# Hybrid encoder layer with product-key retrieval: bank stores on another queue, merged one-hots, token pairs in the weight bank, and 48 spilled up tiles for 60

## The chip, the cores and the metric

One core of a Trainium2 chip. The metric is the device time of one execution in microseconds; lower is better. Engines are called PE (matrix), DVE (vector), ACT (scalar), POOL (GpSimd) and SP (the engine that only issues transfers).

## What is computed

One layer of an encoder on 512 tokens of width 1,024 with 16 meta tokens in front: differential attention and a bidirectional gated linear attention side by side, an output projection, and then a retrieval block (PEER) over 128 x 128 = 16,384 single-neuron experts. Cut to the block that matters here:

```
q = (xn @ w_q)                       # 8 heads x 2 halves of 128
s = q . sub_keys                     # 128 scores per head and half
ts, ti = top_k(s, 16)                # per half
best = top_k(ts0[:, None] + ts1[None, :], 16)      # 16 of 256 pairs
idx = ti0 * 128 + ti1                # expert of each pair
act = gelu(xn . u[idx])
h = h + sum((softmax(best) * act) * v[idx])
```

followed by a final RMS norm. `u` and `v` are 16,384 x 1,024.

## The kernel before

Everything is float32; large products run as three matmuls on a high and a low half (`mm3`, L126 to L129). The first 128 tokens take the **sparse** way: their 128 (head, rank) pairs are fetched row by row from `u` and `v` by indirect transfers that POOL issues (`gather`, L249; 256 in all), and DVE does a dot product per row of `u` (L265) and a multiply-add per row of `v` (L263). The other 384 tokens (three tiles of 128) take the **dense** way: for each of the 128 blocks of 128 experts an *up tile* computes gelu(`u` block . tokens) with 24 matmuls of 384 columns (`u_tile`, L1044), and a *value tile* multiplies it by the gate weights of that block and accumulates with 18 matmuls of 512 columns into six PSUM banks (`v_tile`, L1065 to L1084). The gate weights of all experts for all 384 tokens are built beforehand as a table, the **weight bank** `W_d` in memory.

The stages, in order: the front (attention, projections), the scores and top-16 searches (`topk2`, L189 to L244), and then

- the **bank stage** (loop at L1122 to L1139): `wbuild` builds the bank while the first LA = 60 up tiles run between its pieces, their gelus spilled to memory as `A_d` (L1057). For 8 tokens at a time `prep` (L970) makes one-hots: `L993` compares the two expert indices of each pair with a row 0..127 (two instructions of 1,024 elements), L994 and L996 multiply the first one-hot with the low and the high half of the gate; in every fourth block ACT makes the high product instead (eight instructions at L999). For each token two matmuls of 128 columns (L1021, L1022) sum the outer products over the 128 pairs; four tokens fill one PSUM bank, and ACT drains it (L1024) into a staging tile `stg` of [128, 128, 32], token innermost. After 32 tokens the 2 MB tile is stored to `W_d` (L1026); there are two staging tiles and four one-hot tiles. GS0, RA, RV and RUV say how many gathers are started per up tile or value tile (`pull`), and LA how many up tiles lie in this stage;
- the **value stage** (L1142 on): 128 value tiles; behind the 60th each is joined by one up tile, so the last 68 come as pairs.

A streamed up block goes SP load (`raw`, two buffers), ACT cast (`hi`, L114), `lo` subtraction (L116; on POOL in the bank stage, on DVE afterwards), PE. Each engine runs its instructions in the order that the scheduler wrote them; POOL's queue holds the `lo` subtractions and the gather issues, SP's all loads and the bank stores:

```
hi = stm.tile([P, 1024], F32R, name="hi", tag="hi", bufs=bufs)              # L113
nc.scalar.copy(hi, raw)                                                     # L114
lo = stm.tile([P, 1024], F32R, name="lo", tag="lo", bufs=bufs)              # L115
(eng or nc.vector).tensor_sub(lo, raw, hi.bitcast(F32))                     # L116
```

The row 0..127 is loaded to `iof` at L949, into space that the score tiles release, and cast to `ioh`.

Of the kernel before, what the change touches and what calls it, by code (L numbers as in the profile page):

```python
# [49 lines left out]
SC = 16  # L50
# [32 lines left out]
def _emit(ctx, tc, I, out):  # L83
# [105 lines left out]
    def topk2(a, b, sm, cand, tf, eq, zs):  # L189
# [758 lines left out]
    iof = wk.tile([P, NK], F32, name="iof")  # L948
    nc.sync.dma_start(out=iof, in_=I["iota"].to_broadcast([P, NK]))  # L949
# [11 lines left out]
    def wbuild():  # L961
# [8 lines left out]
        def prep(t, m0):  # L970
            if m0 == 0:
# [5 lines left out]
                iT = wk2.tile([P, 2, P], F16, name="iT")  # L977
                nc.scalar.copy(iT, tr[:, 1:3, :])
                gh = wk2.tile([P, P], F16, name="gh")
                nc.vector.tensor_copy(gh, gT)  # L980
                gl = wk2.tile([P, P], F16, name="gl")
                nc.vector.tensor_sub(gl, gT, gh)
                cur[t] = gT, iT, gh, gl
            gT, iT, gh, gl = cur[t]
            sh = [P, OB // QI, NK, QI]
# [19 lines left out]
        for n, (t, m0) in enumerate(steps):  # L1005
# [262 lines left out]
```

## Time and profile before

| | |
|---|---|
| three timed runs | 1680.73, 1678.32, 1671.53 us; median 1678.32 |
| the profiled execution | 1682.47 us, span of its instructions 1680.7 us |
| busy share of the span | PE 94%, DVE 77%, ACT 44%, POOL 40% |
| memory traffic | 387.42 MB, mean 231 GB/s |
| bank stage, first to last bank matmul | 566.7 to 814.0 us |
| first value matmul | 846.2 us |

The profile is of one execution. Matmuls are pipelined and their ends are modelled, so the distance from one start to the next tells PE's pace. A row that gives "idle before" names what the engine waited for last.

### The profile page before, as it was taken

To read this page: it belongs to the slowest core of one execution; us is meant where nothing else is said; L and a number is where in the kernel's file an instruction comes from. 1 tells how busy PE (TensorE), PEld (TensorE's weight loads), DVE (VectorE), ACT (ScalarE), POOL (GpSimd) and SP (SyncE) were. 2 spreads that over 40 slices of the span, in tenths; PEclk is the share of its full clock that TensorE was granted. 3 is DMA by queue.
4 is the path that set the end of the run, shared out by engine and by line. 5 is a ranking of instruction groups with operands and counts; after the bars stand their busy time and mean duration, and the time that the engine had idled before them with its cause. 6 is when DMAs were issued, how large, how long until landed. Compare 5 with 4: busy or idle time off the path is not lost.

```text
span 1680.7 us, 24243 instructions
## 1 busy us (share of the span) xinstructions
PE 1574.4 (94%) x8793; PEld 1392.4 (83%) x8793; DVE 1291.4 (77%) x2529; ACT 739.6 (44%) x1229; POOL 677.1 (40%) x465
## 2 busy tenths in 40 slices
PE   6999998989986789979989999999999999999998
PEld 6888886768876689878978888889999999988996
DVE  3888768647999998948247777778887888778777
ACT  5454555543324474867533333333333333333334
POOL 3443112076334467475411212154545444344442
PEclk9999999989997989999999999999999999999999
DMA  6112222232224557656999999899999998999885
GB/s 232 54 46 81 69 61 69 84 118 89 78 73 149 176 193 250 239 218 252 328 366 342 326 314 326 278 313 389 321 329 326 336 327 315 319 339 327 308 276 185
DMA packets 152360, 387.42 MB, mean 231 GB/s; under 512 B 12752, under 2 KB 71376, under 8 KB 150576
## 3 DMA queue, kind: packets, MB, share of 16 engines
q1 hardware_dynamic: 106160, 238.79, 41.2%
q0 software_dynamic: 36864, 134.23, 22.8%
q10 hardware_dynamic: 9216, 12.85, 2.1%
q8 instruction: 69, 1.13, 0.3%
q14 instruction: 51, 0.42, 0.1%
HBM read 342.56 MB, written 40.63 MB: 228 GB/s over the span
## 4 chain that ended last, share of the span: by engine, by line
PE 28%; issue 18%; DVE 12%; POOL 10%; DMA 6%; ACT 3%; SPq 1%; POOLq 0%; ACTq 0%; DVEq 0%
POOL gat L251 7%; PE banka L1080 4%; PE banka L1083 4%; PE banka L1084 4%; POOL lo L116 3%; PE bankp L1080 2%; PE bankp L1083 2%; PE bankp L1084 2%; PE bankg L129 2%; DMA gat<-v,idx 2%; PE bankg L127 2%; PE bankg L128 2%; DMA raw<-uT 2%; DVE oh L993 2%; DMA gat<-u,idx 1%
## 5 line engine op out<-in xcount | busy, mean ns | idle before, releaser
L116 POOL TENSOR_TENSOR lo<-raw,hi 128x1024 fp32r<-128x1024 f32 x81 | 238.4, 2947 | 228.8 <-ACT hi L114 220.4
L114 ACT CAST hi<-raw 128x1024 fp32r<-128x1024 f32 x177 | 185.8, 1051 | 289.6 <-PE bankg L128 159.1
L127 PE MATMUL bankg<-un_hi,hi 128*128 128x384 f32 x880 | 300.1, 341 | 12.2 <-ACT act L1055 12.2
L129 PE MATMUL bankg<-un_hi,lo 128*128 128x384 f32 x880 | 299.6, 341 | 5.3 <-POOL lo L116 5.2
L128 PE MATMUL bankg<-un_lo,hi 128*128 128x384 f32 x880 | 297.9, 338 | 0.0
L251 POOL DMA_INDIRECT gat<-u,idx x128 | 157.8, 1232 | 299.5 <-PE bankp L1084 252.1
L251 POOL DMA_INDIRECT gat<-v,idx x128 | 167.8, 1311 | 207.6 <-PE bankp L1084 180.4
L263 DVE SCALAR_TENSOR_TENSOR acc<-gat,sact,acc 128x1024 f32<-128x1024 f32 x128 | 164.2, 1283 | 72.2 <-DMA gat<-v,idx 61.6
L265 DVE CUSTOM_DVE_ANT_0 gat<-gat,hn 128x1024 f32<-128x1024 f32 x128 | 162.9, 1282 | 53.2 <-DMA gat<-u,idx 53.1
L127 PEld LDWEIGHTS bankg<-un_hi,hi 128*128 128x128 f32 x880 | 168.1, 191 | 16.1 <-ACT act L1055 12.5
L135 DVE TENSOR_TENSOR vhl<-vraw,vhl 128x1024 fp32r<-128x1024 f32 x128 | 157.1, 1228 | 30.9 <-ACT vhl L134 30.8
L129 PEld LDWEIGHTS bankg<-un_hi,lo 128*128 128x128 f32 x880 | 167.9, 191 | 8.1 <-POOL lo L116 6.8
L128 PEld LDWEIGHTS bankg<-un_lo,hi 128*128 128x128 f32 x880 | 167.7, 191 | 3.4
L134 ACT CAST vhl<-vraw 128x1024 fp32r<-128x1024 f32 x128 | 134.2, 1049 | 46.3 <-PE bankp L1084 33.4
L116 DVE TENSOR_TENSOR lo<-raw,hi 128x1024 fp32r<-128x1024 f32 x96 | 117.8, 1228 | 24.2 <-ACT hi L114 23.0
L1024 ACT ACTIVATE stg<-banka 128x512 f32<-128x512 f32 x96 | 96.2, 1140 | 1.7 <-PE banka L1022 0.9
L993 DVE TENSOR_TENSOR oh<-iT,ioh 128x1024 f16<-128x1024 f16 x96 | 80.8, 888 | 2.4 <-PE banka L1022 2.4
L1021 PE MATMUL banka<-oh 128*128 128x128 f16 x384 | 55.3, 233 | 22.1 <-DVE oh L996 12.7
L1055 ACT ACTIVATE act<-bankg 128x384 f32<-128x384 f32 x110 | 53.4, 486 | 23.2 <-PE bankg L129 12.1
L1021 PEld LDWEIGHTS <-oh 128*128 128x128 f16 x384 | 39.2, 104 | 20.8 <-DVE oh L996 15.0
L1022 PE MATMUL banka<-oh 128*128 128x128 f16 x384 | 54.3, 233 | 0.7 <-DVE oh L994 0.7
L129 PE MATMUL bankp<-un_hi,lo 128*128 128x384 f32 x144 | 48.7, 338 | 4.5 <-POOL lo L116 4.5
(2283 smaller groups left out, 3906.3 us busy)
## 6 DMA issues: line engine op xcount, KB each, us to landing
raw<-uT SPq DMA_DIRECT2D x128, 512.0 KB
vraw<-v SPq DMA_DIRECT2D x128, 512.0 KB
W_d<-stg SPq DMA_DIRECT2D x12, 2048.0 KB
wa<-W_d SPq DMA_DIRECT2D x32, 768.0 KB
A_d<-act ACTq DMA_DIRECT2D x60, 192.0 KB
wa<-A_d SPq DMA_DIRECT2D x15, 768.0 KB
raw<-wq SPq DMA_DIRECT2D x16, 512.0 KB
raw<-win_n SPq DMA_DIRECT2D x12, 512.0 KB
```

Of the source, the lines that this page charges most:

```text
L114: nc.scalar.copy(hi, raw)
L116: (eng or nc.vector).tensor_sub(lo, raw, hi.bitcast(F32))
L127: nc.tensor.matmul(o, lhsT=ah, rhs=bh, start=start, stop=False)
L128: nc.tensor.matmul(o, lhsT=ah, rhs=bl, start=False, stop=False)
L129: return nc.tensor.matmul(o, lhsT=al, rhs=bh, start=False, stop=stop)
L134: last[0] = nc.scalar.copy(hi, src).ins.name
L135: (eng or nc.vector).tensor_sub(lo, src, hi.bitcast(F32))
L251: g = nc.gpsimd.indirect_dma_start(out=r, out_offset=None, in_=src, in_offset=bass.IndirectOffsetOnAxis(ap=idx[:, hk:hk + 1], axis=0))
L263: nc.vector.scalar_tensor_tensor(acc0, r, sact[:, hk:hk + 1], acc0, op0=ALU.mult, op1=ALU.add)
L265: nc.vector.tensor_tensor_reduce(r, r, hn0, scale=1.0, scalar=0.0, op0=ALU.mult, op1=ALU.add, accum_out=sact[:, hk:hk + 1])
L993: nc.vector.tensor_tensor(o12[:, j], tok(iT[:, j]), ioh[:, None, :, :].to_broadcast(sh), op=ALU.is_equal)
L1080: m0 = nc.tensor.matmul(o, lhsT=gh_[:, tc_], rhs=vh[:, dc], start=(j == 0), stop=False, skip_group_check=True)
```

## The change

Five edits and four numbers.

1. **Stores.** The twelve stores of `stg` go to ACT's queue instead of SP's.
2. **Index row.** `iof` lives in a tile of its own from the start of the retrieval block, and is loaded ahead of `keys`. The score tiles `sc` lose one buffer (SC 16 to 15).
3. **One-hots.** The two compares become one instruction of 2,048 elements; the gate halves lie beside each other in `gs`, and the low and the high product become one instruction of 2,048 elements, except in every fourth block. In `topk2` the two positions and the row 0..15 are bf16, so the compare reads 16-bit operands only.
4. **Bank.** A PSUM bank holds [2, 128, 2] instead of [4, 128]: two adjacent tokens lie beside each other, so a matmul writes every other word, and the drain writes pairs of adjacent words into `stg`.
5. **Numbers.** RA 0.4 to 0.15, RUV 2.85 to 2.7, LA 60 to 48.

```diff
-SC = 16
+SC = 15
-RA = 0.4
+RA = 0.15
-RUV = 2.85
-LA = 60
+RUV = 2.7
+LA = 48
...
-            nc.vector.tensor_tensor(eq, pos[:, :, :, None].to_broadcast([P, PH, TOPK, TOPK]),
-                                    io16[:, None, None, :].to_broadcast([P, PH, TOPK, TOPK]), op=ALU.is_equal)
+            nc.vector.tensor_tensor(eq, pos[:, :, :, None].to_broadcast([P, PH, TOPK, TOPK]),
+                                    io16b[:, None, None, :].to_broadcast([P, PH, TOPK, TOPK]), op=ALU.is_equal)
...
+    iof = w1.tile([P, NK], F32, name="iof")
+    nc.sync.dma_start(out=iof, in_=I["iota"].to_broadcast([P, NK]))
     keys = qs.tile([P, 2 * PH, NK], F32, name="keys")
...
-            for j in range(2):
-                nc.vector.tensor_tensor(o12[:, j], tok(iT[:, j]), ioh[:, None, :, :].to_broadcast(sh), op=ALU.is_equal)
-            nc.vector.tensor_mul(ol, o12[:, 0], tok(gl))
-            if m0 // OB % DM < DN:
-                nc.vector.tensor_mul(od, o12[:, 0], tok(gh))
+            nc.vector.tensor_tensor(o12, tok(iT[:, blk].rearrange("p j m -> p (j m)")),
+                                    ioh[:, None, :, :].to_broadcast([P, 2 * GQ, NK, QI]), op=ALU.is_equal)
...
+            if blk % DM < DN:
+                nc.vector.tensor_mul(oh[:, 2 * GQ:].rearrange("p (c g) k q -> p c (g k q)", c=2).rearrange("p c (g k q) -> p c g k q", k=NK, q=QI),
+                                     o12[:, None, 0].to_broadcast([P, 2] + sh[1:]),
+                                     gs[:, blk].rearrange("p c (g q) -> p c g q", q=QI)[:, :, :, None, :].to_broadcast([P, 2] + sh[1:]))
             else:
+                nc.vector.tensor_mul(ol, o12[:, 0], tok(gs[:, blk, 1]))
...
-                b = bank((P, 4, NK))
+                b = bank((P, 2, NK, 2))
...
-                    nc.tensor.matmul(b[:, q2, :], lhsT=w_, rhs=od[:, m_[0], :, m_[1]], start=True, stop=False)
-                    nc.tensor.matmul(b[:, q2, :], lhsT=w_, rhs=ol[:, m_[0], :, m_[1]], start=False, stop=True)
+                    nc.tensor.matmul(b[:, q2 // 2, :, q2 % 2], lhsT=w_, rhs=od[:, m_[0], :, m_[1]], start=True, stop=False)
+                    nc.tensor.matmul(b[:, q2 // 2, :, q2 % 2], lhsT=w_, rhs=ol[:, m_[0], :, m_[1]], start=False, stop=True)
                 qq = q0 + 4 * g_
-                nc.scalar.activation(stg[:, :, qq:qq + 4].rearrange("p i n -> p n i"), b, AF.Copy, scale=1.0 / GS)
+                nc.scalar.activation(stg[:, :, qq:qq + 4].rearrange("p i (a n) -> p a i n", n=2), b, AF.Copy, scale=1.0 / GS)
             if q0 + OB == BL:
-                nc.sync.dma_start(out=W_d[:, ((t - 1) * P + m0) // BL], in_=stg)
+                nc.scalar.dma_start(out=W_d[:, ((t - 1) * P + m0) // BL], in_=stg)
```

The scheduler writes the order anew. On SP, from the score weights to the bank stage, `raw<-uT` being the loads of up blocks, before:

```order
L897 DMA keys<-keys 128x2048
L108 DMA raw<-wq 128x1024 x11
L108 DMA raw<-uT 128x1024 x7
L949 DMA iof<-iota 128x128
L108 DMA raw<-uT 128x1024 x14
L1026 DMA W_d<-stg 128x4096
L108 DMA raw<-uT 128x1024 x3
```

and with the change:

```order
L901 DMA iof<-iota 128x128
L903 DMA keys<-keys 128x2048
L108 DMA raw<-wq 128x1024 x11
L108 DMA raw<-uT 128x1024 x47
L1050 DMA vraw<-v 128x1024 x2
L1122 DMA wa<-W_d 128x12x128
```

Nothing stands between the up loads of the bank stage any more; the first loads of the value stage (`vraw`, `wa`) follow them.

On ACT the first store of the bank now stands behind the drains (`stg`) and ahead of the next gelu (`act`) and cast (`hi`):

```order
L1066 ACTIVATE act<-bankg 128x384
L1035 ACTIVATE stg<-banka 128x2x128x2 x2
L1068 DMA A_d<-act 128x384
L1035 ACTIVATE stg<-banka 128x2x128x2 x6
L1037 DMA W_d<-stg 128x4096
L1066 ACTIVATE act<-bankp 128x384
L114 CAST hi<-raw 128x1024
```

On DVE, at the start of the bank stage, the one-hots (`oh`), an index chain (`eq`) and uses of gathered rows (`gat`), before:

```order
L993 TENSOR_TENSOR oh<-iT,ioh 128x1024 x7
L996 TENSOR_TENSOR oh<-oh,gh 128x1024
L994 TENSOR_TENSOR oh<-oh,gl 128x1024
L265 ISA gat,sact<-gat,hn_70 128x1024
L265 ISA sact 128x1
L994 TENSOR_TENSOR oh<-oh,gl 128x1024
L996 TENSOR_TENSOR oh<-oh,gh 128x1024
```

and with the change:

```order
L234 TENSOR_TENSOR eq<-sm_cb,io16b 128x2048
L228 TENSOR_TENSOR sm_cf<-sm_cf,sm_bsv 128x128
L230 TENSOR_SCALAR sm_rf<-sm_rf 128x128
L985 CAST gs<-gT 128x16x8
L999 TENSOR_TENSOR oh<-iT,ioh 128x2048 x4
L236 TENSOR_TENSOR eq<-eq,tf 128x2048
L229 TENSOR_TENSOR sm_cb<-sm_cf,sm_t_6099 128x128
L231 TENSOR_TENSOR sm_rb<-sm_rf,sm_t_6099 128x128
L986 TENSOR_TENSOR gs<-gT,gs 128x16x8
L237 TENSOR_TENSOR eq<-eq 128x128x8
L1004 TENSOR_TENSOR oh<-oh,gs 128x2048 x3
L1008 TENSOR_TENSOR oh<-oh,gs 128x1024
```

Half as many one-hot instructions do the same elements; four uses of gathered rows stand in this stage instead of sixteen, and the third of the four index chains has moved ahead of the first one-hot but for its second half. On PE the new order has 410 up matmuls ahead of the first bank matmul, 598 between it and the last, and 144 behind that; before, the 144 were the same and the first two numbers 377 and 919.

## Rows read from the trace of the kernel before

**Rows 1.** Busy time by stage: stretch, its length, then busy us (and instructions) of PE, its weight loads, DVE, ACT and POOL, the granted clock of PE, the DMA share and GB/s. The stretches are the bank stage, the way to the first value matmul, and the value stage up to and behind the point where pairs begin.

```profile
566.70:814.10 247.40, 216.76 (x1670) 207.06 (x1669) 202.62 (x231) 171.06 (x268) 149.88 (x52) 0.95 0.65 233
814.10:846.10 32.00, 25.15 (x147) 24.83 (x144) 5.25 (x6) 10.50 (x16) 10.41 (x5) 0.96 0.99 349
846.10:1124.50 278.40, 278.32 (x1241) 232.61 (x1242) 204.05 (x297) 101.94 (x141) 60.68 (x58) 0.99 0.93 321
1124.50:1672.70 548.20, 545.39 (x2769) 494.70 (x2767) 441.80 (x523) 193.58 (x278) 246.78 (x183) 1.00 0.90 318
```

**Rows 2.** PE in order of time: start, duration, line, operation and tiles, count, and in brackets the idle time before it with what ended it. All bank matmuls between the third and the fourth row follow without a gap.

```profile
508.82 0.69 PE L127 MATMUL bankg<-un_hi,hi 128*128 128x384 f32 x1 [12.16 <-ACT act L1055]
...
517.65 0.48 PE L974 MATMUL bankp<-ident,sel 128*128 128x128 f32 x1 [5.13 <-DVE sel L243]
...
681.42 0.22 PE L1021 MATMUL banka<-oh 128*128 128x128 f16 x1
...
681.94 0.22 PE L1022 MATMUL banka<-oh 128*128 128x128 f16 x1
...
682.22 0.33 PE L128 MATMUL bankg<-un_lo,hi 128*128 128x384 f32 x1
...
682.57 0.34 PE L127 MATMUL bankg<-un_hi,hi 128*128 128x384 f32 x1
...
846.18 0.79 PE L1080 MATMUL banka<-vhl,gh__8527 128*128 128x512 f32 x1 [6.92 <-ACT gh__8527 L134]
```

**Rows 3.** The bank stage again, PE and its weight loads for line L127 alone (one of the three matmuls of an up step), then clock, DMA share and GB/s.

```profile
566.70:814.10 247.40, 103.14 (x299) 57.16 (x299) 0.95 0.65 233
```

**Rows 4.** DVE's groups of instructions in the bank stage: line, operation, tiles and shapes, count, busy us, mean ns of one, idle time before them and what ended it.

```profile
L993 DVE TENSOR_TENSOR oh<-iT,ioh 128x1024 f16<-128x1024 f16 x88 | 73.6, 883 | 2.4 <-PE banka L1022 2.4
L994 DVE TENSOR_TENSOR oh<-oh,gl 128x1024 f16<-128x1024 f16 x48 | 43.4, 908 | 0.0
L996 DVE TENSOR_TENSOR oh<-oh,gh 128x1024 f16<-128x1024 f16 x35 | 32.5, 931 | 0.0
L265 DVE CUSTOM_DVE_ANT_0 gat<-gat,hn 128x1024 f32<-128x1024 f32 x16 | 27.4, 1712 | 35.8 <-DMA gat<-u,idx 35.8
L233 DVE TENSOR_TENSOR eq<-eq,tf 128x2048 bf16<-128x2048 bf16 x4 | 7.0, 1739 | 0.1
L234 DVE TENSOR_TENSOR eq<-eq 128x1024 bf16<-128x1024 bf16 x4 | 6.9, 1727 | 0.1
L231 DVE TENSOR_TENSOR eq<-sm_cf,io 128x2048 bf16<-128x2048 f32 x2 | 4.6, 2286 | 0.0
L231 DVE TENSOR_TENSOR eq<-sm_rf,io 128x2048 bf16<-128x2048 f32 x2 | 4.6, 2277 | 0.0
```

**Rows 5.** Who waited for whom in the bank stage: engine, tile and line, what it waited for, us in total, times, the longest.

```profile
DVE gat L265 <- DMA gat<-u,idx: 35.8, 6, 8.5
ACT hi L114 <- DMA raw<-uT: 32.4, 11, 5.5
```

**Rows 6.** SP's queue in order of time: start, time from the first to the last issue of the row, line, transfer, count.

```profile
447.36 32.63 SPq L108 DMA_DIRECT2D raw<-uT  x7
501.37 0.33 SPq L949 DMA_DIRECT2D iof<-iota  x1
...
578.73 0.33 SPq L1026 DMA_DIRECT2D W_d<-stg  x1
```

**Rows 7.** DVE in order of time, columns as for PE.

```profile
506.13 0.29 DVE L950 CAST ioh<-iof 128x256 f16<-128x256 f32 x1 [2.23 <-DMA iof<-iota]
...
583.73 1.21 DVE L233 TENSOR_TENSOR eq<-eq,tf 128x2048 bf16<-128x2048 bf16 x1
...
679.58 1.28 DVE L993 TENSOR_TENSOR oh<-iT,ioh 128x1024 f16<-128x1024 f16 x2
680.79 2.88 DVE L994 TENSOR_TENSOR oh<-oh,gl 128x1024 f16<-128x1024 f16 x1
```

**Rows 8.** POOL in order of time.

```profile
680.73 2.39 POOL L116 TENSOR_TENSOR lo<-raw,hi 128x1024 fp32r<-128x1024 f32 x1 [0.24 <-ACT hi L114]
...
742.60 12.51 POOL L116 TENSOR_TENSOR lo<-raw,hi 128x1024 fp32r<-128x1024 f32 x1 [2.64 <-ACT hi L114]
```

**Rows 9.** ACT's groups in the bank stage, columns as for DVE.

```profile
L1024 ACT ACTIVATE stg<-banka 128x512 f32<-128x512 f32 x94 | 94.1, 1139 | 1.7 <-PE banka L1022 0.9 <-ACT act L1055 0.8
L114 ACT CAST hi<-raw 128x1024 fp32r<-128x1024 f32 x39 | 41.1, 1055 | 43.0 <-DMA raw<-uT 32.4 <-PE banka L1022 5.6 <-POOL lo L116 3.2
L999 ACT ACTIVATE oh<-oh,gT 128x128 f16<-128x128 f16 x93 | 29.3, 427 | 31.7 <-DVE oh L993 31.6
```

**Rows 10.** A drain of the same size with a contiguous output, from the groups of the whole execution.

```profile
L928 ACT COPY pq<-banka 128x512 f32<-128x512 f32 x16 | 9.3, 582 | 0.0
```

**Rows 11.** ACT in order of time: the issue of a gelu's store, and the gelus of two up tiles that follow each other in the value stage.

```profile
700.49 0.33 ACTq L1057 DMA_DIRECT2D A_d<-act  x1
...
1199.30 0.48 ACT L1055 ACTIVATE act<-bankg 128x384 f32<-128x384 f32 x1
...
1207.60 0.49 ACT L1055 ACTIVATE act<-bankg 128x384 f32<-128x384 f32 x1
```

**Rows 12.** The first part of the value stage, PE and its weight loads for line L1080 alone; six of them make a value tile.

```profile
846.10:1124.50 278.40, 147.23 (x374) 71.02 (x374) 0.99 0.93 321
```

**Rows 13.** POOL's largest group in the bank stage.

```profile
L116 POOL TENSOR_TENSOR lo<-raw,hi 128x1024 fp32r<-128x1024 f32 x38 | 132.9, 3502 | 92.4 <-ACT hi L114 84.1 <-PE banka L1022 8.2
```

More of the change, by code (lines that the diff above doesn't have):

```diff
@@ L155, in _emit @@
     io16 = cst.tile([P, TOPK], F32, name="io16")
+    io16b = cst.tile([P, TOPK], BF, name="io16b")
     def half(name, tag, j, n):
@@ L218, in topk2 @@
         cf = sm("cf")
+        rb = sm("rb", BF)
+        cb = sm("cb", BF)
         nc.vector.tensor_copy(rf, row)
@@ L225, in topk2 @@
         nc.vector.tensor_add(cf, cf, t1)
-        nc.vector.tensor_sub(cf, cf, t9)
+        nc.vector.tensor_sub(cb, cf, t9)
         nc.vector.tensor_scalar(rf, rf, -1.0, 0.0, op0=ALU.add, op1=ALU.max)
-        nc.vector.tensor_add(rf, rf, t9)
+        nc.vector.tensor_add(rb, rf, t9)
         yield
-        for j, pos in enumerate((rf, cf)):
+        for j, pos in enumerate((rb, cb)):
             nc.vector.tensor_tensor(eq, pos[:, :, :, None].to_broadcast([P, PH, TOPK, TOPK]),
-                                    io16[:, None, None, :].to_broadcast([P, PH, TOPK, TOPK]), op=ALU.is_equal)
+                                    io16b[:, None, None, :].to_broadcast([P, PH, TOPK, TOPK]), op=ALU.is_equal)
             nc.vector.tensor_mul(eq, eq, tf[:, :, j, None, :].to_broadcast([P, PH, TOPK, TOPK]))
@@ L361, in _emit @@
     nc.sync.dma_start(out=io16, in_=I["iota"][:, :TOPK].to_broadcast([P, TOPK]))
+    nc.vector.tensor_copy(io16b, io16)
     ropc = fx("ropc", [P, TM], "ropc")
@@ L947, in _emit @@
     ioh = wk.tile([P, NK, QI], F16, name="ioh")
-    iof = wk.tile([P, NK], F32, name="iof")
-    nc.sync.dma_start(out=iof, in_=I["iota"].to_broadcast([P, NK]))
     nc.vector.tensor_copy(ioh, iof[:, :, None].to_broadcast([P, NK, QI]))
@@ L976, in prep @@
                 nc.scalar.activation(gT, tr[:, 0, :], AF.Copy, scale=GS)
[L977 to L985, printed above, removed]
@@ L995, in prep @@
-            if m0 // OB % DM < DN:
-                nc.vector.tensor_mul(od, o12[:, 0], tok(gh))
+                iT = wk2.tile([P, P // OB, 2, OB], F16, name="iT")
+                nc.scalar.copy(iT.rearrange("p b j m -> p j b m"), tr[:, 1:3, :].rearrange("p j (b m) -> p j b m", m=OB))
+                gs = wk2.tile([P, P // OB, 2, OB], F16, name="gs")
+                g8 = gT.rearrange("p (b m) -> p b m", m=OB)
+                nc.vector.tensor_copy(gs[:, :, 0, :], g8)
+                nc.vector.tensor_sub(gs[:, :, 1, :], g8, gs[:, :, 0, :])
@@ new lines, in prep @@
+                cur[t] = gT, iT, gs
+            gT, iT, gs = cur[t]
+            GQ = OB // QI
+            sh = [P, GQ, NK, QI]
+            def tok(v):
+                n = v.shape[1] // QI
+                return v.rearrange("p (g q) -> p g q", q=QI)[:, :, None, :].to_broadcast([P, n, NK, QI])
+            oh = big.tile([P, 4 * GQ, NK, QI], F16, name="oh", tag=("hi0", "hi1", "lo0", "lo1")[(t * P + m0) // OB % WB])
+            o12 = oh[:, :2 * GQ]
+            blk = m0 // OB
+            nc.vector.tensor_tensor(o12, tok(iT[:, blk].rearrange("p j m -> p (j m)")),
+                                    ioh[:, None, :, :].to_broadcast([P, 2 * GQ, NK, QI]), op=ALU.is_equal)
```

5 lines of the change are left out of this document (2 added, 3 removed).

## The prediction

> **What bounds the kernel now.** I read the busy time by stage first, then DVE, PE and ACT inside the one stage that the change rebuilds, then the queues.
>
> The table by stage [rows 1] shows PE at 278.3 of 278.4 and 545.4 of 548.2 us in the two parts of the value stage: there PE sets the time, and whatever lies beside it is hidden. In the bank stage (first to last bank matmul, 247.4 us) PE is busy for 216.8 by modelled ends, but its work is less. Nine bank matmuls follow each other from 681.42 to 681.94, 0.058 us each, and two up matmuls from 682.22 to 682.57, 0.175 each [rows 2]; 299 rows of one of the three up lines [rows 3] make 897 up matmuls, so 897 x 0.175 + 768 x 0.058 = 157 + 45 = 202 us. PE has 45 us to spare.
>
> DVE has none: busy 202.6 us [rows 1], and of the rest 35.8 us waiting for the gathers of the sparse part [rows 4, 5], together 238 of 247. **DVE paces the bank stage**, half of its loss being gathers that arrive late. They are late because POOL issues them behind its `lo` subtractions, which wait for ACT's `hi` casts, which wait for `raw<-uT` (32.4 us in this stage [rows 5]), which SP issues behind `W_d<-stg` stores that wait for a full staging tile [rows 6]. A second loss is the lock between DVE and POOL: a one-hot instruction takes 0.68 us alone (1.28 for two) and 2.88 when a POOL `lo` of 2.39 us starts just ahead of it [rows 7, 8]; the other way round one `lo` lasted 12.51 us.
>
> **The change part by part.** The sum is made against the profiled execution, span 1680.7, its own time 1682.47; the median of the three timed runs, 1678.32, lies 4.1 lower.
>
> *Index row and bf16 compares, before the bank.* SP issued `iof` only at 501.37, 21 us after the up load ahead of it (447.36 + 32.63 = 480.0) [rows 6], and the up loads behind it waited as long; PE stood 12.16 us at 508.82 [rows 2]. That stall goes, but PE's next wait in order, for DVE's `sel` at 517.65 (5.13 us), grows by as much, since DVE lost only 2.23 us by `iof` [rows 7]. DVE gains these 2.23 us and about 1.07 us on each of four compares (2.28 in f32; I take 1.21, the multiply of the same size on bf16 operands [rows 4, 7]): 6.5 us. Against it, the new order puts one more index chain, about 4.5 us (1.21 each for compare and multiply, less for each fold), ahead of the first one-hot. Net **-2 us**, bounds -8 and +4.
>
> *One-hots.* 171 instructions of 0.68 us = 116 us become 84 of double size and 12 single ones. The price of the double form is not in the trace; between 1.21 (bf16 multiply of 2,048 elements, the nearest row) and 2.28 (f32 compare) [rows 4, 7] I take 1.21: 84 x 1.21 + 12 x 0.68 = 110, so **-6**. The upper end would be +84.
>
> *Lock.* Measured one-hot time is 73.6 + 43.4 + 32.5 = 149.5 [rows 4], so 33.5 us were waits, 0.88 for each of 38 `lo` [rows 13]. The new order has 598 up matmuls between first and last bank matmul, 25 tiles: 22 us, **-11.5**. Bounds 0 and -22.
>
> *Gathers.* RA falls, and 16 uses in the stage become 4 in the new order. One cost 1.71 busy and 2.24 waiting (27.4 and 35.8 over 16 [rows 4]): 12 x 3.95 = **-47.4**. With no more waiting at all it would be -56; if only the busy part left, -21. The 12 others go to the value stage, into DVE's free time there (441.8 of 548.2 busy [rows 1]); per up-and-value pair there are fewer than before, 2.7 for 2.85.
>
> *Index chains.* Four in the stage become two whole ones and the rest of a third: compares 9.2 to 2.4, multiplies 7.0 to 5.2, first folds 6.9 to 5.2 [rows 4]: **-10**.
>
> *Drain.* The drain L1024, whose writes lie 128 bytes apart, takes 1.139 us, a contiguous one of the same size 0.582 [rows 9, 10]. Pairs lie between; I take 0.6, saving 52 us on ACT. On the path this is worth nothing by itself (ACT's waits are long), but it is the cover for the rest: with 96 drains, 25 `hi` casts of 1.055, 25 gelus of 0.48 and the 96 quarter products (29.3 busy for 93) [rows 9, 11] ACT needs 58 + 26 + 12 + 30 = 126 us; at 1.139 it would need 177.
>
> *Stores on ACT's queue.* Twelve issues at the 0.33 us of an `A_d` issue, which runs beside ACT's work [rows 11]: nothing, at most 4 us. Behind a store stand ACT's next gelu and cast; it waits only for ACT's own last drain.
>
> *Bank matmuls.* Their output now skips every other word of the PSUM row. No row shows such a matmul: the low end is 0.058, the high end twice that, as the strided drain cost twice the contiguous one. The nearest row is the same matmul with the same operands, so 0.058: PE needs 598 x 0.175 + 45 = 150 us.
>
> PE's load is then 150 of some 175 and DVE will stand at a full ring of four one-hot buffers more often than the few us of now: **+6**, bounds 0 and +15.
>
> Stage: 247.4 - 6 - 11.5 - 47.4 - 10 + 6 = **178.5**, so -69.
>
> *LA 60 to 48.* Twelve up tiles move to the value stage, where PE is full: 24 x 0.175 = 4.2 us each. From the other side a pair takes 8.30 (1199.30 to 1207.60 [rows 11]) and a value-only tile 278.4 / (374 / 6) = 4.47 with the few up tiles in it [rows 1, 12], which leaves 3.83. I take 4.2: **+50**. Twelve `A_d` stores and their loads vanish unseen.
>
> *Between the stages* 144 up matmuls and the way store, load, split follow the last bank matmul in both orders: 32 us with 6.92 of waiting [rows 1, 2], unchanged. So is the tail.
>
> Sum: -2 - 69 + 50 = -21: a run like the profiled one takes 1661, a median some 4 less. Forecast **1658 us**.
>
> [...]
>
> **The rivals.**
>
> *PE becomes the bound (chance 0.30; slower).* If a bank matmul with a skipping output takes 0.116, 768 of them take 89 us, PE needs 105 + 89 = 194, and with 13 to 23 of its present 45 us of loss the stage lasts 207 to 217: +8 to +18, a median of about 1689. For it: the doubled drain shows that a pattern over words can halve a rate; against it: PE reads its operands at a stride already and keeps 0.058. It decides from about 0.10 us per matmul, where with 18 us of loss the stage reaches the 199 at which the change gains nothing. With every PE gap closed the sum would be -5.
>
> *The drain stays at 1.139 (0.08; no change).* ACT needs 177 and loses 15 more waiting: stage 192, sum -7, 1671.
>
> *POOL starves (0.10; no change).* Longer DVE instructions leave fewer openings; if the waits of `lo` (12.51 in one case [rows 8]) come twice as often, up tiles are late and PE loses 20 us: stage 198, sum -1, 1677.
>
> [...]
>
> **How the numbers follow.** Forecast 0.47: 0.42 faster, 0.05 same. About 0.5%, 8.4 us, is what a measurement of this kernel tells from no change. PE bound: 0.03 faster, 0.12 same, 0.15 slower. Drain: 0.02 faster, 0.05 same, 0.01 slower. POOL: 0.03 faster, 0.05 same, 0.02 slower. Double form: slower 0.03 and same 0.02. Together: faster 0.50, same 0.29, slower 0.21. The likeliest case alone spans 1642 (lock and gather waits at their good ends) to 1672. The range goes up to the PE case: **1642 to 1690**.
>
> **What would show it.** First bank matmul near 565, last near 743; DVE's gather wait in the stage under 10 us; no up load behind `iof` or a store on SP; `stg` at 0.6 us; the double one-hots at 1.2; bank matmuls still 0.058 apart; the first value matmul near 775 and 877 us to the last. Bank matmuls 0.11 apart, or a bank stage over 200 us, make the forecast wrong.

## The result, and the profile after

The changed kernel takes **1697.37 us** (median of 4) against 1678.52 of the kernel before: ratio 1.0124, 95% interval 1.0091 to 1.0157 (ratios and intervals are taken over all runs, so they are not the quotient of two medians). The forecast was 1658 in a range of 1642 to 1690: wrong in sign, and outside the range. The profiled execution has a span of 1696.3, 15.6 above 1680.7.

The stages after, columns as in [rows 1]: up to the first bank matmul, the bank stage, the way to the first value matmul, the value stage (its row ends at 1687.92, the last value matmul starts at 1688.38).

```profile
470.00:578.74 108.74, 75.64 (x414) 74.43 (x414) 108.54 (x438) 36.09 (x53) 41.13 (x17) 0.87 0.31 105
578.74:778.17 199.43, 188.50 (x1348) 183.24 (x1347) 152.28 (x118) 117.39 (x238) 86.53 (x30) 0.97 0.59 218
778.17:808.53 30.36, 25.31 (x148) 24.99 (x146) 4.95 (x7) 9.04 (x14) 9.13 (x4) 1.00 0.99 349
808.53:1687.92 879.39, 875.35 (x4293) 776.32 (x4294) 672.21 (x854) 310.61 (x439) 318.62 (x253) 1.00 0.88 311
```

Against before: the first bank matmul comes 12.0 us later (566.74), the stage is 48 shorter, the way between 2 shorter, the value stage 53 longer. In the bank stage PE's own work is now 574 up matmuls x 0.1735 and 768 bank matmuls x 0.109, 183 of 199 us (202 of 247 before): PE is now the fullest engine, and DVE is busy for 152. (The prediction took 598 up matmuls for this stage; the trace has 574, since one tile's 24 run only after the first value matmul.)

PE in order of time, columns as in [rows 2]: two stalls, and the middle of the stage.

```profile
520.61 0.47 PE L978 MATMUL bankp<-ident,sel 128*128 128x128 f32 x1 [21.61 <-DVE sel L246]
...
607.54 0.39 PE L1032 MATMUL banka<-oh 128*128 128x128 f16 x1 [10.93 <-DVE oh L1004]
...
681.31 0.31 PE L1032 MATMUL banka<-oh 128*128 128x128 f16 x1
...
682.40 0.31 PE L1032 MATMUL banka<-oh 128*128 128x128 f16 x1
```

From the third row to the fourth it is ten bank matmuls: **0.109 us each, for 0.058** [rows 2]. The first row is the stall ahead of the bank: one of 21.61 now, where 12.16 and 5.13 stood [rows 2]. The second row is a new stall at the start of the stage.

DVE's groups in the bank stage, and below them ACT's drain; columns as in [rows 4].

```profile
L999 DVE TENSOR_TENSOR oh<-iT,ioh 128x2048 f16<-128x2048 f16 x44 | 70.1, 1615 | 8.6 <-PE banka L1033 8.6
L1004 DVE TENSOR_TENSOR oh<-oh,gs 128x2048 f16<-128x2048 f16 x35 | 52.1, 1517 | 0.1
L1008 DVE TENSOR_TENSOR oh<-oh,gs 128x1024 f16<-128x1024 f16 x12 | 12.4, 1037 | 0.1
L268 DVE CUSTOM_DVE_ANT_0 gat<-gat,hn 128x1024 f32<-128x1024 f32 x4 | 4.9, 1216 | 13.7 <-DMA gat<-u,idx 13.7
L234 DVE TENSOR_TENSOR eq<-sm_rb,io16b 128x2048 bf16<-128x2048 bf16 x1 | 2.3, 2277 | 0.0
```

```profile
L1035 ACT ACTIVATE stg<-banka 128x512 f32<-128x512 f32 x95 | 57.8, 632 | 35.2 <-PE banka L1033 34.8
```

Four gathers for 16 [rows 4], 0.63 us a drain for 1.139 [rows 9], double one-hots whose median is 1.21 (the rows give means, which hold the longer ones beside a POOL `lo`, up to 3.42): as the prediction has them. But the compare of the index chain (`eq`, L234) takes 2.28 in bf16 as it did in f32.

What delays the start: DVE in order of time (index chains that now stand ahead of the first one-hots), then POOL beside them and at the first gather.

```profile
551.50 2.26 DVE L234 TENSOR_TENSOR eq<-sm_rb,io16b 128x2048 bf16<-128x2048 bf16 x1
...
560.70 2.47 DVE L240 TENSOR_TENSOR sel<-eq 128x128 f32<-128x128 bf16 x1
...
563.50 2.27 DVE L234 TENSOR_TENSOR eq<-sm_cb,io16b 128x2048 bf16<-128x2048 bf16 x1
565.71 2.48 DVE L228 TENSOR_TENSOR sm_cf<-sm_cf,sm_bsv 128x128 f32<-128x128 f32 x1
568.11 2.42 DVE L230 TENSOR_SCALAR sm_rf<-sm_rf 128x128 f32<-128x128 f32 x1
...
570.59 4.62 DVE L999 TENSOR_TENSOR oh<-iT,ioh 128x2048 f16<-128x2048 f16 x4
```

```profile
560.14 2.77 POOL L116 TENSOR_TENSOR lo<-raw,hi 128x1024 fp32r<-128x1024 f32 x1 [9.77 <-ACT hi L114]
563.84 6.61 POOL L116 TENSOR_TENSOR lo<-raw,hi 128x1024 fp32r<-128x1024 f32 x2 [0.93 <-ACT hi L114]
578.70 12.84 POOL L116 TENSOR_TENSOR lo<-raw,hi 128x1024 fp32r<-128x1024 f32 x1 [8.25 <-DVE oh L1004]
591.71 1.15 POOL L254 DMA_INDIRECT gat<-u,idx  x1 [0.17 <-issue]
```

Six of the eight index compares now run ahead of the first one-hot, four before; the three short instructions at 560.70, 565.71 and 568.11, of 0.2 to 0.4 us at their shortest, took 2.4 to 2.5 beside a POOL `lo`. The first one-hot starts at 570.59; before, it was 558.78. Then one `lo` lasted 12.84 us, the gather behind it was issued at 591.71, DVE waited 13.7 us for it and PE 10.93 for DVE.

**PE idle**, below, is a stage's length less PE's work in it: up matmuls (the row's count of PE instructions less 768 bank matmuls and 6 transposes) x 0.1735, and 768 bank matmuls x 0.058 or 0.109. Before: 247.3 - 155 - 44.5 = 48 us. After: 199.4 - 574 x 0.1735 - 83.7 = 16. It takes in what a lowered clock costs: before, 590 to 594 and 620 to 625 are stretches with a granted clock of 0.50.

### The profile page after: what moved, and what is told of

The parts are those of the page before. It is cut to its first block, busy times and chain, and to the rows that moved or that the text cites. A ratio compares the mean times of both kernels' runs of the same rounds, so it can differ in the third digit from the quotient of the medians.

```text
span 1696.3 us, 24079 instructions
## 1 busy us (share of the span) xinstructions
PE 1605.0 (95%) x8793; PEld 1423.8 (84%) x8793; DVE 1278.4 (75%) x2458; ACT 703.5 (41%) x1229; POOL 629.6 (37%) x453
## 4 chain that ended last, share of the span: by engine, by line
PE 26%; issue 24%; DVE 11%; POOL 10%; DMA 6%; ACT 1%; SPq 1%; POOLq 0%; ACTq 0%; DVEq 0%
POOL gat L254 10%; DMA gat<-u,idx 2%; PE banka L1091 2%; PE banka L1032 2%; PE banka L1033 2%; PE banka L1094 2%; PE banka L1095 2%; PE bankg L128 2%; PE bankg L127 2%; PE bankg L129 2%; DMA gat<-v,idx 2%; PE bankp L1094 1%; PE bankp L1095 1%; PE bankp L1091 1%; PE banka L127 1%
## 5 line engine op out<-in xcount | busy, mean ns | idle before, releaser
L127 PE MATMUL bankg<-un_hi,hi 128*128 128x384 f32 x912 | 307.1, 337 | 0.0
L129 PE MATMUL bankg<-un_hi,lo 128*128 128x384 f32 x912 | 306.7, 336 | 0.0
L128 PE MATMUL bankg<-un_lo,hi 128*128 128x384 f32 x912 | 306.1, 336 | 0.0
L116 POOL TENSOR_TENSOR lo<-raw,hi 128x1024 fp32r<-128x1024 f32 x69 | 191.3, 2774 | 259.8 <-ACT hi L114 242.1
L266 DVE SCALAR_TENSOR_TENSOR acc<-gat,sact,acc 128x1024 f32<-128x1024 f32 x128 | 164.0, 1281 | 84.4 <-DMA gat<-v,idx 83.7
L268 DVE CUSTOM_DVE_ANT_0 gat<-gat,hn 128x1024 f32<-128x1024 f32 x128 | 155.8, 1220 | 66.2 <-DMA gat<-u,idx 66.2
L127 PEld LDWEIGHTS bankg<-un_hi,hi 128*128 128x128 f32 x912 | 171.8, 188 | 3.9
L116 DVE TENSOR_TENSOR lo<-raw,hi 128x1024 fp32r<-128x1024 f32 x108 | 132.4, 1227 | 15.7 <-ACT hi L114 14.7
L1032 PE MATMUL banka<-oh 128*128 128x128 f16 x384 | 89.2, 315 | 15.1 <-DVE oh L1004 15.1
L1033 PE MATMUL banka<-oh 128*128 128x128 f16 x384 | 89.9, 317 | 0.0
L999 DVE TENSOR_TENSOR oh<-iT,ioh 128x2048 f16<-128x2048 f16 x48 | 74.7, 1581 | 8.6 <-PE banka L1033 8.6
L1035 ACT ACTIVATE stg<-banka 128x512 f32<-128x512 f32 x96 | 58.3, 632 | 35.2 <-PE banka L1033 34.8
L1032 PEld LDWEIGHTS <-oh 128*128 128x128 f16 x384 | 51.7, 135 | 16.0 <-DVE oh L1004 11.2
L1033 PEld LDWEIGHTS <-oh 128*128 128x128 f16 x384 | 51.9, 135 | 4.4 <-issue 4.4
```

The source lines that it names most:

```text
L127: nc.tensor.matmul(o, lhsT=ah, rhs=bh, start=start, stop=False)
L128: nc.tensor.matmul(o, lhsT=ah, rhs=bl, start=False, stop=False)
L129: return nc.tensor.matmul(o, lhsT=al, rhs=bh, start=False, stop=stop)
L266: nc.vector.scalar_tensor_tensor(acc0, r, sact[:, hk:hk + 1], acc0, op0=ALU.mult, op1=ALU.add)
L268: nc.vector.tensor_tensor_reduce(r, r, hn0, scale=1.0, scalar=0.0, op0=ALU.mult, op1=ALU.add, accum_out=sact[:, hk:hk + 1])
L1032: nc.tensor.matmul(b[:, q2 // 2, :, q2 % 2], lhsT=w_, rhs=od[:, m_[0], :, m_[1]], start=True, stop=False)
```

## The experiments

Rows are of the bank stage, columns as in [rows 1]; ratios are to the kernel before. The letters of theories are those of the expectations.

**1. The pairs alone.** These four have the order of the kernel they come from on every engine. First, contiguous matmuls and the old drain.

```diff
-                b = bank((P, 2, NK, 2))
+                b = bank((P, 4, NK))
-                    nc.tensor.matmul(b[:, q2 // 2, :, q2 % 2], ...)
+                    nc.tensor.matmul(b[:, q2, :], ...)
-                nc.scalar.activation(stg[...].rearrange("p i (a n) -> p a i n", n=2), b, ...)
+                nc.scalar.activation(stg[...].rearrange("p i n -> p n i"), b, ...)
```

> The changed kernel with the bank tile contiguous again (four tokens one after the other), and so the drain with its 128-byte stride again; the order on every engine stays as it is. Theory P, the bank matmul takes 0.109 us because its output skips every other word: 0.058 here, PE's work in the bank stage 574 x 0.1735 + 45 = 144 us, drain 1.14 us (ACT 117 + 49 = 166), DVE 152 busy and 27 waiting; stage 175 to 190 for 199.4, time 1672 to 1687. Theory Q, it is the new one-hot tile (both products by one instruction, read by the matmul at the same stride but from elsewhere): the matmul stays at 0.109, only the drain gets dearer: 1697 to 1705. Theory R, the matmul is dearer but does not set the stage, the stalls at its start do (gather 13.7 us, chain 13.7 us): 0.058, and the stage stays at 195 to 200: 1692 to 1698.

Next, contiguous matmuls as in the first, with the drain still writing pairs. Its diff is shown for the drain alone.

```diff
-                nc.scalar.activation(stg[...].rearrange("p i (a n) -> p a i n", n=2), b, ...)
+                nc.scalar.activation(stg[...].rearrange("p i (a n) -> p a i n", n=2),
+                                     b.rearrange("p (a n) i -> p a i n", n=2), ...)
```

> The changed kernel with the bank tile contiguous for the matmuls, while the drain still writes pairs: it now reads PSUM at a stride (two tokens 512 bytes apart) and writes two adjacent words. Theory P: matmul 0.058; if the drain's time is set by what it writes, 0.63 us, ACT as before the edit (117 busy), stage 170 to 185, time 1667 to 1682; if reading at a stride costs as much as writing at one, drain 1.14 and the time that of the contiguous bank, 1672 to 1687. Theory Q: 0.109 and 1694 to 1700.

Third, the opposite edit: the kernel before with the pairs.

> The kernel before with the pairs alone (bank tile of two adjacent tokens, drain of pairs); order unchanged. Theory P: bank matmul 0.109, PE's work in the bank stage 157 + 84 = 241 us for 202, while DVE with its gathers still fills 238 of 247: the stage grows by a part of 39, to 255 to 285, time 1686 to 1716; drain 0.63. Theory Q: matmul 0.058, drain 0.63, ACT 48 us less busy, which was not what the stage waited for: 1670 to 1680.

Fourth, four adjacent tokens instead of two.

```diff
-                b = bank((P, 2, NK, 2))
+                b = bank((P, NK, 4))
-                    nc.tensor.matmul(b[:, q2 // 2, :, q2 % 2], ...)
+                    nc.tensor.matmul(b[:, :, q2], ...)
-                nc.scalar.activation(stg[...].rearrange("p i (a n) -> p a i n", n=2), b, ...)
+                nc.scalar.activation(stg[...], b, ...)
```

> The changed kernel with the bank in groups of 128 columns by four adjacent tokens: the matmul writes every fourth word (16 bytes apart) instead of every second. [...] If the price grows with the stride: 0.21, PE's work in the stage 574 x 0.1735 + 768 x 0.21 = 261, stage 270 to 280, time 1768 to 1780. The drain writes runs of 16 bytes, 0.58 to 0.63.

Measured, in this order: 1693.1 (1.0085, 1.0057 to 1.0112); 1688.3 (1.0043, 1.0022 to 1.0065); 1683.6 (1.0021, 1.0001 to 1.0041); 1696.8 (1.0123, 1.0075 to 1.0170). PE with contiguous matmuls and pairs in the drain (nine between the rows), and with four tokens (ten):

```profile
681.85 0.22 PE L1032 MATMUL banka<-oh 128*128 128x128 f16 x1
...
682.36 0.22 PE L1033 MATMUL banka<-oh 128*128 128x128 f16 x1
```

```profile
679.87 0.31 PE L1032 MATMUL banka<-oh 128*128 128x128 f16 x1
...
680.96 0.31 PE L1032 MATMUL banka<-oh 128*128 128x128 f16 x1
```

The matmul goes from 0.109 to 0.057 with the output alone: theory P on the cause is shown, Q is out. Four words apart cost the same 0.109 as two: the price did not grow with the stride. The stages of the contiguous bank with the old drain, of the contiguous one with pairs, and of before with pairs:

```profile
586.90:761.90 175.00, 157.62 (x1350) 149.82 (x1349) 152.45 (x112) 148.55 (x233) 82.24 (x29) 0.95 0.66 243
```

```profile
578.53:764.58 186.05, 157.95 (x1348) 150.82 (x1347) 151.96 (x118) 111.12 (x236) 98.90 (x29) 0.94 0.62 230
```

```profile
562.84:811.03 248.19, 242.41 (x1669) 235.49 (x1669) 215.76 (x228) 136.42 (x264) 136.60 (x55) 1.00 0.68 238
```

But theory P missed the size: of its ranges for the time, the first three runs met none. The first run's 1693.1 lies in theory R's, but its stage does not: 175.0 us, begun 8 us later and ended 16 us earlier than in the change. The matmuls cost 39 us more work; the stage changes by 13.4 (186.0 to 199.4), the median by 9.1, for PE idle is 42 without pairs and 16 with them. In the kernel before, whose PE had 48 us to spare, 39 us of work vanish nearly whole (idle 9, stage +0.9). And without the doubled matmul the change is *still slower* than before. The drain on the same matmuls, with pairs and with its old writes:

```profile
L1035 ACT ACTIVATE stg<-banka 128x512 f32<-128x512 f32 x94 | 52.8, 643 | 18.0 <-PE banka L1033 17.5 <-ACT act L1066 0.4
```

```profile
L1035 ACT ACTIVATE stg<-banka 128x512 f32<-128x512 f32 x93 | 93.1, 1145 | 4.0 <-PE banka L1033 2.5 <-ACT act L1066 1.2
```

0.643 us when it reads PSUM 512 bytes apart and writes pairs, 1.145 when its writes lie 128 bytes apart. The first bank matmul came between 578.5 and 589.6 in runs of this one order; the ends compare better than the starts.

**2. The drain alone**, in the kernel before; and, in the change with contiguous matmuls and pairs in the drain, the stores' queue.

```diff
-                nc.scalar.activation(stg[...].rearrange("p i n -> p n i"), b, ...)
+                nc.scalar.activation(stg[...].rearrange("p i (a n) -> p a i n", n=2),
+                                     b.rearrange("p (a n) i -> p a i n", n=2), ...)
```

> The kernel before with the drain alone changed: it reads its contiguous bank tile at a stride and writes pairs, 0.63 us for 1.139; matmuls and order as before. If ACT's load is off the path (DVE and the gathers pace the stage): stage 243 to 248, time 1672 to 1680. If the long drains made the casts and so the gathers late: DVE's gather wait falls from 35.8 to under 20, stage 227 to 237, time 1660 to 1670.

```diff
-                nc.scalar.dma_start(out=W_d[...], in_=stg)
+                nc.sync.dma_start(out=W_d[...], in_=stg)
```

> The changed kernel with contiguous bank matmuls, the drain writing pairs, LA = 48, and the stores of the bank on SP's queue again. The run with them on ACT's queue gave 1688.3. If the queue decides nothing (the up loads wait for a free buffer anyway): 1685 to 1692. If a store that waits for a full staging tile keeps the up loads back: PE loses 5 to 12 us in the bank stage, 1693 to 1700.

Measured: 1678.9 (1.0000, 0.9976 to 1.0023), stage 241.3; 1685.7 against 1688.3, last bank matmul at 764.6 in both. By the time, the 41 us that the drains save on ACT and the choice of queue are both off the path, as forecast. The stage lies between the two ranges of the first expectation: the gather wait fell from 35.8 to 20.0 and the last bank matmul came 5 us earlier, which the medians don't show.

**3. The plan's numbers alone**, in the kernel before: `LA` 60 to 48, then the gather ratios too (`RA` 0.4 to 0.15, `RUV` 2.85 to 2.7).

> The kernel before with LA = 48 alone (gather ratios stay at 0.4 and 2.85; eleven gather uses in the bank stage, four compares ahead of the first one-hot). Theory S: the stage is paced by DVE, whose work falls by five gathers and a third of the locks (5 x 3.95 + 8 = 28 us at most), while 56 us of PE work leave it for the value stage, where PE is full: stage 215 to 240, PE's idle time there 60 to 90, time 1698 to 1722. If the stage shrinks with its PE work: 1675 to 1685.

> The kernel before with the three numbers of the plan alone (LA 48, RA 0.15, RUV 2.7): its order then has six compares ahead of the first one-hot, four gather uses in the bank stage and as many up tiles there as the changed kernel. The prediction's terms for these: index chain +2 to +8, gathers -47, lock -11, LA +50: 1666 to 1680. Theory S (time is PE's work plus PE's idle): PE's work in the stage falls from 202 to 145, DVE's from 239 to 195 to 205 with its waits, so PE's idle time stays near 50 while the value stage grows by 53 and the first bank matmul comes 8 to 12 us later: 1688 to 1700, slower.

Measured: **1693.9** (1.0108, 1.0065 to 1.0151) and **1705.8** (1.0167, 1.0133 to 1.0200). Stage and DVE's gather group with LA alone, then the same two rows with all three numbers, and for these three of PE's waits, from 470 us to the end of the stage (us in total, times, the longest):

```profile
569.64:770.76 201.12, 169.01 (x1379) 158.90 (x1379) 178.97 (x220) 148.10 (x236) 119.46 (x36) 0.94 0.61 229
```

```profile
L265 DVE CUSTOM_DVE_ANT_0 gat<-gat,hn 128x1024 f32<-128x1024 f32 x11 | 18.3, 1662 | 10.8 <-DMA gat<-u,idx 10.8
```

```profile
578.87:781.39 202.52, 167.93 (x1353) 158.10 (x1352) 150.02 (x199) 150.59 (x237) 116.27 (x29) 0.89 0.57 214
```

```profile
L265 DVE CUSTOM_DVE_ANT_0 gat<-gat,hn 128x1024 f32<-128x1024 f32 x4 | 7.3, 1834 | 14.9 <-DMA gat<-u,idx 14.9
```

```profile
PE banka L1021 <- DVE oh L996: 19.2, 7, 4.3
PE bankg L129 <- POOL lo L116: 16.9, 5, 5.4
...
PE banka L1021 <- ACT stg L1024: 3.7, 8, 1.9
```

LA alone shortens the stage by 46 and lengthens the value stage by 49 (826.5 to 875.5): a trade, and a loss with what comes beside it. My expectation missed, 215 to 240 for its stage and 1698 to 1722 for the time; all three numbers came out above theory S's 1688 to 1700 and far above the 1666 to 1680 of the prediction's terms. With LA alone the gather wait falls from 35.8 to 10.8 already. The stage has 26 `lo` for 38 on POOL, where the gathers are issued, but that this is the reason isn't shown: with the pairs alone, at 39 `lo`, the wait is 7.8. With the ratios too, seven more gathers leave, DVE is busy 29 us less (179 to 150, 11 of them gathers), and the stage does **not** get shorter: PE idle is 52, then 58. What does change is the order: six compares ahead, first bank matmul at 578.9 for 569.6.

**4. LA back at 60 in the changed kernel**, with contiguous matmuls and with the change's; and the old gather ratios at LA = 48, with contiguous matmuls.

> The changed kernel with contiguous bank matmuls, the drain writing pairs (as in the run of the strided read), and LA back at 60; its order has four compares ahead of the first one-hot (six at LA = 48) and five gather uses in the bank stage. Theory S, the time is PE's work plus PE's idle time, so where the twelve up tiles stand does not matter by itself, but they fill what the stage leaves idle: work 157 + 45 = 202 us covers DVE's 159 busy and its waits, idle falls from 43 to 15 to 20, first bank matmul near 566, last near 786, then 32 + 826 + 8: 1645 to 1660. Theory T, the 43 us of PE idle in the run without the pairs come from DVE and POOL waiting on each other and stay: stage 245, time 1676 to 1682.

> The changed kernel (pairs kept) with LA back at 60; same order as the run beside it that has no pairs. Theory S: PE's work in the stage 157 + 84 = 241, idle 10 to 18, first bank matmul near 566, last near 820, then 32 + 826 + 8: 1680 to 1690, 30 to 39 above the run without the pairs, since PE is the bound there. Theory T: idle stays at 18 or more and the first bank matmul at 579: 1696 to 1702.

> The changed kernel with contiguous bank matmuls, the drain writing pairs, LA = 48, and the ratios of gathers back at 0.4 and 2.85: ten gather uses in the bank stage for four, and four compares ahead of the first one-hot for six. Theory S: first bank matmul 8 to 12 us earlier (566 to 571); DVE gains six uses, 7 us busy and up to 13 waiting; stage 190 to 205 for 186; the value stage stays PE's (882): 1676 to 1694. If gathers in the stage cost only where DVE has no idle time, stage 186 and time 1674 to 1678.

Measured: 1692.1 (1.0073), 1707.1 (1.0167), 1690.4 (1.0059): the first two far off the expectation, the third inside theory S's. The last use of a gather and the last value matmul of the first, and the stage of the third:

```profile
1677.57 1.28 DVE L266 SCALAR_TENSOR_TENSOR acc<-gat,sact,acc 128x1024 f32<-128x1024 f32 x1 [0.46 <-DMA gat<-v,idx]
```

```profile
1664.98 0.39 PE L1095 MATMUL bankp<-vhl,gl__15104 128*128 128x512 f32 x1
```

```profile
569.57:770.29 200.72, 169.69 (x1376) 160.99 (x1376) 175.84 (x140) 115.20 (x239) 106.80 (x36) 0.90 0.62 231
```

PE was done at 1665.0, earlier than before (1672.7), and the gathers left over held the end to 1694. With 68 pairs instead of 80, 2.7 gathers a pair don't get through 256. The first bank matmul came at 569.9, 566.8 and 569.6, all with four compares ahead. The third has 11 gather uses in its stage for the change's four: its last bank matmul comes 6 us later than with the change's ratios (770.3 for 764.6), its value stage is 5 shorter (876.9 for 881.8), and the times are the same within their noise (1690.4 and 1688.3).

**5. The same without the tail**: LA = 60 and `RUV` = 3.0, contiguous matmuls, drain of pairs. Then LA = 72 and 3.6; the first with the pairs back; the first with single one-hots.

> The changed kernel with contiguous bank matmuls, the drain writing pairs, LA = 60, and 3.0 gathers per up-and-value pair for 2.7. In the run with 2.7 the last value matmul came at 1665.0 and then 29 us of gathers followed. Theory S: they now end with the value stage, 8.5 us follow the last value matmul: 1668 to 1680. If three gathers a pair are more than DVE or the DMA queues can take beside PE, the pairs get longer than 8.30 us: 1685 to 1700.

> As the run with LA = 60 and 3.0 gathers per pair, with LA = 72 and 3.6. Theory S: twelve more up tiles (50 us of PE work) go into the bank stage, 252 us of work there cover DVE's 159 busy and 28 waiting, idle falls from 29 to 10 to 15; last bank matmul near 832, then 32 + 776 + 8: 1645 to 1660. If idle time does not come from too little PE work but from DVE and POOL waiting on each other at every up tile (more splits, more locks), it stays at 29 or grows, and 3.6 gathers a pair crowd DVE: 1670 to 1690.

> The changed kernel (pairs kept) with LA = 60 and 3.0 gathers per pair: beside the run at 1661 without the pairs it differs in the bank matmul's output alone, with the same order on every engine. If PE's idle time in the bank stage (30 us there) takes up most of the 39 us that the matmuls get longer, as it did with 12.8 us between the two runs with a gather tail: 1670 to 1678. If PE is the bound of that stage and all of the 39 shows: 1695 to 1700. If the pairs cost nothing once the plan is right: 1658 to 1665.

```diff
-            nc.vector.tensor_tensor(o12, tok(iT[:, blk]...), ioh...to_broadcast([P, 2 * GQ, NK, QI]), op=ALU.is_equal)
+            for j in range(2):
+                nc.vector.tensor_tensor(o12[:, j * GQ:(j + 1) * GQ], tok(iT[:, blk, j]), ..., op=ALU.is_equal)
...
-                nc.vector.tensor_mul(oh[:, 2 * GQ:]..., o12[:, None, 0]..., gs[:, blk]...)
+                nc.vector.tensor_mul(ol, o12[:, 0], tok(gs[:, blk, 1]))
+                nc.vector.tensor_mul(od, o12[:, 0], tok(gs[:, blk, 0]))
```

> The kernel of the run at 1661 with the one-hots taken apart again (one instruction of 1,024 elements each, 0.68 us, for the double one of 1.21); LA = 60, 3.0 gathers, contiguous bank matmuls and drain of pairs stay. DVE's one-hots are then 180 x 0.68 = 122 us for 110, but a POOL subtraction that starts beside one holds it for less (in the kernel before 41 us of excess over all one-hots, in the run at 1661 49): DVE needs 0 to 12 us more, PE's idle time in the stage is 30: 1658 to 1670. If the double form were what makes the stage short, 1670 to 1680.

Measured: **1661.2** (0.9893, 0.9861 to 0.9926), faster than both kernels and 7 us below my range; 1687.1 (1.0034, 1.0006 to 1.0062); 1676.9 (0.9997, 0.9968 to 1.0025); 1674.2 (0.9967, 0.9942 to 0.9991). Stages in this order (under that of LA = 72 its gather group on DVE):

```profile
565.03:793.23 228.20, 210.26 (x1668) 202.95 (x1668) 191.91 (x130) 129.07 (x263) 121.57 (x45) 0.97 0.66 236
```

```profile
567.40:840.10 272.70, 259.08 (x1956) 251.86 (x1955) 195.36 (x131) 147.23 (x285) 152.90 (x59) 0.98 0.66 234
```

```profile
L268 DVE CUSTOM_DVE_ANT_0 gat<-gat,hn 128x1024 f32<-128x1024 f32 x8 | 15.4, 1920 | 64.9 <-DMA gat<-u,idx 64.9
```

```profile
564.92:806.62 241.70, 240.99 (x1667) 235.82 (x1667) 185.00 (x130) 135.85 (x265) 119.47 (x46) 1.00 0.63 225
```

```profile
565.30:803.87 238.57, 215.14 (x1670) 206.55 (x1670) 182.87 (x206) 128.50 (x260) 136.91 (x45) 0.96 0.62 225
```

With LA at 60 the one-hots, the gathers and the drain shorten the stage by 19 and nothing is given back. Pairs add 13.5 there (15.7 of the median, same order on every engine), as expected where PE's idle time takes up most of the 39. Single one-hots add 10.4 to the stage, though DVE's busy time falls by 9: its gather wait grows from 9.7 to 23.8. That run also has another order, so part of it may be the order's. LA = 72 missed theory S: 50 us more of PE work made the stage 44.5 longer, DVE waited 64.9 us for gathers, and the last gather's use came 23 us after the last value matmul at 1646.0.

## Why the prediction was wrong

Two steps failed: the price of the bank matmul (0.058 taken, 0.109 measured) and the way to the first bank matmul (-2 forecast, +12 measured). The gathers' term was wrong as a mechanism, but the stage's other terms came within 8 us as a sum: 186.0 with contiguous matmuls, for 178.5.

The stage ladder, from the profiled runs; the last column is the median of the timed runs (that of the kernel before was 1678.5 to 1680.0 beside them).

| kernel | first bank matmul | bank stage | between | value stage | PE idle in the stage | median |
|---|---|---|---|---|---|---|
| before | 566.7 | 247.3 | 32.2 | 826.5 | 48 | 1678.5 |
| LA = 48 alone | 569.6 | 201.1 | 35.6 | 875.5 | 52 | 1693.9 |
| all three numbers | 578.9 | 202.5 | 32.1 | 882.5 | 58 | 1705.8 |
| the change, contiguous matmuls | 578.5 | 186.0 | 31.3 | 881.8 | 42 | 1688.3 |
| the change | 578.7 | 199.4 | 30.4 | 879.8 | 16 | 1697.4 |

Read down the last column: the three numbers cost 27 us, the other edits without the strided matmul give 17 back (one-hots, chains and drain; stores and index row show no gain of their own), and the pairs on the matmuls cost 9 again.

- **Bank matmuls: the step that failed by my own ranking.** "The nearest row is the same matmul with the same operands, so 0.058"; they took 0.109. The row had the operands but not the output, which was the thing changed. The first rival had it (0.116, stage 207 to 217): it gave the price well, but the stage came out at 199.4, where by its own sum the change gains and loses nothing. That it had the sign right is partly luck: the 12 us at the start, which no rival had, decided it. The runs give the size: 0.109 with an output that skips words for 0.057 without, a factor of 1.9 for two words as for four.
- **It is 13 of a miss of 36.** Against the sum of -21 the profiled run stands at +15.6: 14 before the bank, 21 in the stage (13.4 of them the matmuls), 3 in the value stage, less 2 between.
- **Before the bank: the other step that failed, -2 forecast with bounds -8 and +4, +12 measured.** The bf16 compare gained nothing (2.28, not 1.21). Its `sm_rb` is broadcast along the innermost axis; the operands of the multiply (1.21) are not, nor are those of the one-hot compare L999 of the same size (median 1.21). No run changes the broadcast alone, so that it is the reason is not shown. And I priced one more index chain at 4.5; there went one and a half, 2.26 for each compare, and three short instructions took some 2 us longer each beside a POOL `lo`. The plan's three numbers together do it, not the other edits: 578.9 with them alone, 563 to 570 in all ten runs with LA at 60 or 72 or with the old ratios.
- **Gathers, -47.4, and lock, -11.5: 59 forecast, 45 measured for the three numbers together, and not by these terms.** I used "DVE paces" as though every us off DVE came off the stage. LA alone, with five gathers and twelve `lo` fewer, is worth 20 + 11 by these terms and took 46; the seven other gathers, worth 28, took nothing in the kernel before, and in the change with contiguous matmuls the 6 us by which they end the stage earlier come back in the value stage (5). Once DVE had 150 of 202, PE waited for one-hots (19.2 us), `lo` (16.9) and drains (3.7) in turn, with no engine full. The lock, as I call it when a DVE instruction takes longer beside a POOL `lo`: the excess of all one-hots over their median times fell from 40 to 33 us, with 25 `lo` for 38; with the three numbers alone, also 25 `lo` but single one-hots, it is 24. Such a lock makes either form some 2.2 us longer (0.68 becomes 2.88, 1.21 becomes 3.42).
- **LA, +50: right** (+53 measured), but it was read as a price for something. It buys nothing: PE is full in the value stage, so an up tile costs its 4.2 us there. With LA alone the bank stage lost 46 us and the value stage gained 49. The sum -69 + 50 hid that most of the -69 was what leaves with those same tiles.
- **One-hots, chains, ring: -10 forecast, -16.5 measured** (202.5 to 186.0, with the drain's help; the double form has a median of 1.21 in the change, and no run shows the slow one to which I gave 0.03 slower and 0.02 same); **drain 0.6: right** (0.632), off the path as said; **stores: right**, nothing.
- **Index row: right for PE.** The up loads run without a break from 449.72, and PE's stall moved into the next wait: 21.61 for 17.29. The 2.23 us that DVE was to gain don't show: its third compare starts at 523.77, for 521.92 before.

```profile
449.72 101.01 SPq L108 DMA_DIRECT2D raw<-uT  x17
```

What is not settled: which wait keeps PE idle at LA = 48 with contiguous matmuls (52 and 58 us in part 3, where DVE is busy for 179 and 150; 31 with the old drain and 42 with pairs in part 1). The waits listed in part 3 are spread over DVE's one-hots, POOL's `lo` and ACT, and a version with no such wait was not tried.

## What to carry to other kernels

Where one stage is full on an engine and another has it idle, the time is that engine's work plus its idle time: work that moves from the idle stage to the full one is paid in full, and a gain in the idle stage that needs this move is no gain. Keep the work where it is covered, take the DVE gains there, and see that what is pushed out of the stage (here the ten gathers that leave it at LA = 60) still fits in the next (3.0 a pair, not 2.7). A layout that speeds up one end of a buffer has two ends: here pairs took the drain from 1.139 us to 0.632, and the matmul from 0.058 to 0.109. Let the engine with slack do the strided side (ACT reading PSUM at a stride, 0.643) and leave the matmul's output contiguous (0.057).

## What was not expected of the hardware

- The doubling is nearly the same at both clock levels. At a granted clock of 0.50 the bank matmul took 0.107 us contiguous (before, 28 of them from 621.03 to 624.02) and 0.213 with a skipping output (after, 607.5 to 610, behind the idle time of 10.93); at 1.00 it took 0.058 and 0.109.
- The mean granted clock of the bank stage goes with PE's idle time: 0.89 to 0.96 in the stages with 31 to 58 us of it, 1.00 in the four with under 10 (pairs on the kernel before, LA = 60 with pairs twice, four tokens). In part this is so by reckoning, since PE idle holds what the low clock costs. An estimate from these rows, if the clock is always either 0.50 or 1.00: a mean of 0.95 over 247 us is 25 us at half speed, some 12 of the 48 us before; with the pairs alone the clock stayed at 1.00, so these 12 are part of why 39 us of extra work showed so little.
- ACT's drain takes 1.139 us when its SBUF writes lie 128 bytes apart, 0.632 in runs of 8 bytes, 0.595 in runs of 16 (four adjacent tokens), and a contiguous one of another line 0.582 [rows 10]; reading PSUM 512 bytes apart added 0.01.
- One POOL `lo`, 2.40 us at the median, took 12.84: it started at 578.70, DVE worked without a gap until 589.3, and it ended 2.3 us after that. Everything queued behind it on POOL, the first gather too (issued at 591.71), waited as long.
